# Putting off three quarters of the first-level picks, and putting the low weight part on the one-hots with ScalarE

## The chip, the core and the metric

The kernel runs on one core of one Trainium2 chip. The metric is the device time of one execution in microseconds. Three executions of the kernel before gave 1546.49 (median), 1546.44 and 1548.01 us.

## The reference, cut to what matters

One encoder layer over 512 tokens of width 1024: attention (two kinds), a LayerNorm, and a retrieval feed-forward (PEER) beside a gated embedding, then a second LayerNorm. The change is in the feed-forward:

```python
q = (xb @ w_q).reshape(PEER_CHUNK, PEER_HEADS, PEER_KEY_DIM)
s1 = jnp.einsum('thd,kd->thk', q[..., :half], sub_keys[0])
s2 = jnp.einsum('thd,kd->thk', q[..., half:], sub_keys[1])
v1, i1 = lax.top_k(s1, PEER_TOPK)
v2, i2 = lax.top_k(s2, PEER_TOPK)
cand = (v1[..., :, None] + v2[..., None, :]).reshape(PEER_CHUNK, PEER_HEADS, PEER_TOPK * PEER_TOPK)
cv, ci = lax.top_k(cand, PEER_TOPK)
...
g = jax.nn.softmax(cv.astype(jnp.float32), axis=-1).reshape(PEER_CHUNK, -1).astype(xb.dtype)
u = u_table[idx]
hpre = jnp.einsum('td,ted->te', xb, u)
act = g * jax.nn.gelu(hpre, approximate=False)
return jnp.einsum('te,ted->td', act, v_table[idx])
```

There are 8 heads, 128 sub-keys on each of two sides, 16 picks for each head, and 16384 experts; so every token has 128 experts with a weight each.

## The kernel before, in words

The 512 tokens are four chunks of 128: chunk 0, chunk 1 (`NGC`), chunks 2 and 3. Chunk 0 gathers its experts' rows by indirect DMA (GpSimd issues them). Chunks 1 to 3 become a dense matrix of weights (token by expert), which is multiplied with all of the value table; the activations of chunks 2 and 3 come from dense "lead" products with the u table (`lead_block`, L1156), those of chunk 1 from gathered rows (`own_rows`).

The stages around the change, in order:

- **Query stage.** For each of 16 groups g (a head and a side), TensorE projects all tokens (L113 to L115) and scores them against the 128 sub-keys (`sub_scores`, L849). ScalarE copies the scores of the four chunks out in one instruction (L858), and VectorE picks the 16 best for each chunk at once (`top16`, L831: five instructions, called a pick below; 64 picks in all).
- **Lead stage.** TensorE works through a fixed list, `gate_and_leads`: 100 lead blocks of 8 matmuls and, among the first, 16 gate steps of 12. VectorE, meanwhile: `route(1)` (second-level picks and the indices), `route(2)`, `build_g(2)`, `route(3)`, `build_g(3)`, `route(0)`, `build_g(1)`. The 128 gathered rows of chunk 1 (`own_rows`, L1071: one instruction each on 128x1024, the gather five buffers ahead, L1069) are strewn between the steps from `route(2)` on, and 26 rows of chunk 0 (`beside`) among and after `build_g(1)`.
- **build_g** turns a chunk's picks into dense weights. Three transposes (L993) on TensorE bring indices and weights into place, and VectorE copies them out (L997). Then there are 16 steps of 8 tokens. VectorE makes the one-hots of both indices (L1041) and multiplies one of them by the weight's upper and lower 16-bit part (L1052, two instructions); TensorE multiplies the pairs (L1016), ScalarE copies the sums out (L1028, two instructions). Every fourth step ScalarE issues a write of 2 MB to DRAM (L1033): 12 writes over the three builds.
- **Value stage.** 128 blocks, each read, cut in two parts and multiplied with the weights (L1389), beside the other gathers of chunk 0.

All five engines follow an order that is fixed while the program is recorded. The vector steps `yield` an amount of us; `run` gives that amount times `PACE` (1.1) of lead work to TensorE (`run_pe`) and times `OWN` of gathered rows to VectorE. So the amounts decide which lead matmuls stand ahead of which transposes in TensorE's list, and the gate's lower parts (`g_lo`, L1185) stand in VectorE's list where the lead work called for them. The one-hot tiles (`oh_i`, `oh_j`) have two buffers.

Of the kernel before, what the change touches and what calls it, by code (L numbers as in the profile page):

```python
# [9 lines left out]
F32 = mybir.dt.float32  # L10
F32R = mybir.dt.float32r
I32 = mybir.dt.int32
F16 = mybir.dt.float16
U32 = mybir.dt.uint32
AF = mybir.ActivationFunctionType
OP = mybir.AluOpType
# [17 lines left out]
GT = 32  # L34
GB = 8
LEAD = 100
SPILL = 88
KEPT = 8
FIRST = 8
PACE = 1.1  # L40
AHEAD = 14.0
LAG = 6.0
BESIDE = 26
PRE = BESIDE
OWN = 1.2
OWN_G = 0.7
OWN_G_LATE = 4.0
SEAM = 7.0
# [3 lines left out]
OT = 8  # L52
G_UP = 32768.0
# [18 lines left out]
def tile_encoder_layer(ctx: ExitStack, tc: tile.TileContext, A: dict, out: bass.AP):  # L72
    nc = tc.nc
# [18 lines left out]
    def r32(ap):  # L92
        return ap.bitcast(F32)
# [748 lines left out]
    gb = rw.tile([128, D], F32, name="gb")  # L842
    for k in range(8):
        nc.gpsimd.tensor_tensor(whole[:, k, :], r32(hTh[:, k, ts]), r32(hTl[:, k, ts]), op=OP.add)
    pQ = ExitStack()
    rq = pQ.enter_context(tc.tile_pool(name="rq", bufs=1, reuse_waits="tile"))
    skT = rq.tile([128, 2, 128], F32, name="skT")
    nc.sync.dma_start(skT, A["skT"])
    def sub_scores(g, ps):  # L849

        qT = rq.tile([128, 512], F32, name="q_t", bufs=2)
        nc.scalar.copy(qT, ps)
        pt = ps_tile("tr")
        for c in range(4):
            nc.tensor.matmul(pt[:, c * 128:(c + 1) * 128], qT[:, c * 128:(c + 1) * 128], skT[:, g % 2, :],
                             start=True, stop=True)
        s = rq.tile([128, 4, 128], F32, name="sc", bufs=3)
        nc.scalar.copy(s, pt.rearrange("p (c k) -> p c k", c=4))  # L858
        for c in range(4):
            tmp = rq.tile([128, 128], F32, name="tk_t", bufs=2)  # L860
            top16(v_all[:, c, g // 2, g % 2], i_all[:, c, g // 2, g % 2], s[:, c, :], tmp)

    first = []
    for g in range(16):
# [20 lines left out]
        sub_scores(g, ps)  # L885
    pQ.close()

    pb = ExitStack()
    bt = pb.enter_context(tc.tile_pool(name="bt", bufs=2, side="right", reuse_waits="tile"))
    bs = [pb.enter_context(tc.tile_pool(name=f"bs{x}", bufs=1, side="right", reuse_waits="tile")) for x in range(2)]  # L890
    rg = pR.enter_context(tc.tile_pool(name="rg", bufs=1, reuse_waits="tile"))

    def route(c, res):
# [93 lines left out]
    def build_g(c, e1, e2, gw):  # L987
# [9 lines left out]
        nc.vector.tensor_copy(eT.rearrange("p q s t -> p s q t"),  # L997
                              ps[:, 0:256].rearrange("p (s q t) -> p s q t", s=2, t=OT))
        yield 0.4
        wT = bt.tile([128, 2, 128], F16, name="wT")  # L1000
        nc.scalar.mul(wT[:, 0], ps[:, 256:384], G_UP)
        nc.vector.scalar_tensor_tensor(wT[:, 1], ps[:, 256:384], G_UP, wT[:, 0], op0=OP.mult, op1=OP.subtract)
        yield 0.3
        wide = [128, OT // 2, 128, 2]

        def in_pairs(x):
            return x.rearrange("p (a b) -> p a b", b=2).unsqueeze(2)
# [29 lines left out]
        for q in range(128 // OT):  # L1037
            t0 = OT * q

            om = bt.tile([128, 2, OT // 2, 128, 2], F16, name="oh_i")  # L1040
            nc.vector.tensor_tensor(om.rearrange("p s a j b -> p (s a) j b"),  # L1041
                                    iota2.unsqueeze(1).to_broadcast([128, OT, 128, 2]),
                                    in_pairs(eT[:, q].rearrange("p s t -> p (s t)")).to_broadcast([128, OT, 128, 2]),
                                    op=OP.is_equal)
            if ahead:
                sums = products(*ahead)
                due -= 1.3
            yield 1.2

            ow = bt.tile([128, 2, OT // 2, 128, 2], F16, name="oh_j")  # L1050
            for x in range(2):
                nc.vector.tensor_tensor(ow[:, x], om[:, 1], in_pairs(wT[:, x, t0:t0 + OT]).to_broadcast(wide),  # L1052
                                        op=OP.mult)
                if not x:
                    yield 0.65
            if ahead:
                leave(ahead[0], sums)
            ahead = (q, om, ow)
            yield 0.65
        sums = products(*ahead)  # L1060
# [216 lines left out]
    with tc.manual_schedule(engines={nc.vector.engine, nc.scalar.engine, nc.tensor.engine, nc.sync.engine,  # L1277
                                     nc.gpsimd.engine}):
        for _ in range(RAWS):
            load_u()  # L1280
        held = []
        run(route(NGC, held))
        own = own_rows(*held)
        run_pe(next(own))
        own_due = -OWN_LATE
        for c in range(NGC + 1, 4):
            res = []
            run(route(c, res), OWN)
            if c > NGC + 1:
                run_pe(WAIT)  # L1290
            run(build_g(c, *res), OWN)
        lead0 = route(0, [])
        for _ in range(14):
            run([next(lead0)], OWN)
        own_due = 1e9
        run([0.0], 1.0)
        for _ in own:
            pass
        own = None
        run_pe(LAG)  # L1300

        first_g = pX.tile([128, NTG, GB, GT], F32, name="gt1")
        nc.sync.dma_start(first_g[:, 128 // GT:].rearrange("p g i t -> p g (i t)"),
                          g_dram[128 // GT:, :, SPILL * GT:(SPILL + GB) * GT].rearrange("g p x -> p g x"))
        build = build_g(NGC, *held)
        next(build)
        run(lead0)
        own = beside()
        own_due = -OWN_G_LATE
        run(build, OWN_G)  # L1310
        for x in own:
            run_pe(x)
        pb.close()
# [247 lines left out]
```

## Time and profile before

| | |
|---|---|
| median of the runs | 1546.49 us |
| profiled execution, its time | 1548.03 us |
| profiled execution, its span | 1545.9 us |
| mean granted TensorE clock | 0.98 of full speed |
| TensorE busy | 1472.0 us (95%) |
| VectorE busy | 1291.7 us (84%) |
| ScalarE busy | 551.0 us (36%) |
| GpSimd busy | 581.2 us (38%) |
| moved by DMA | 459.34 MB |

Busy shares are means over stages with different limits; the stage that the change touches runs from about 412 us (the first lead matmul) to about 913 us. What is 2 us longer than the span is the start and the end around it. DMA "share" is the mean busy share of 16 DMA engines.

### The profile page before, as it was taken

The numbers are of one execution on the slowest core, as the hardware profiler recorded it, in microseconds if no ns is written. First come the engines' busy times: TensorE is split into PE (matmuls) and PEld (weight loads), VectorE is DVE, ScalarE is ACT, GpSimd is POOL, SyncE is SP. The second block draws the span as 40 slices with busy tenths as digits, with TensorE's granted clock in tenths as the row PEclk, the third lists the DMA queues.
The fourth block names the chain that finished last, engine by engine and source line by source line (L and its number), as shares of the span: only waits on it lengthen the run. The fifth ranks groups of instructions, "written<-read, shape, count | busy, mean of one in ns | idle before, by whom it ended". The sixth has DMA issues, their size and how long they took to land.

```text
span 1545.9 us, 22318 instructions
## 1 busy us (share of the span) xinstructions
PE 1472.0 (95%) x7747; PEld 1219.7 (79%) x7747; DVE 1291.7 (84%) x2737; ACT 551.0 (36%) x938; POOL 581.2 (38%) x520
## 2 busy tenths in 40 slices
PE   9999899999999998998799969999999999999997
PEld 5788777788888887887688747888887888887785
DVE  7376685679889987888688978999998999989996
ACT  3355685333222222212222223434433333333332
POOL 1013110010015434354422454556555666665620
PEclk9999999999999999999999979999999999999999
DMA  6343240143379999999998999999999999999982
GB/s 228 99 113 96 79 123 28 48 139 91 106 240 344 344 394 392 403 412 398 405 357 309 411 379 369 405 403 395 406 400 394 396 395 395 396 395 397 392 329 82
DMA packets 194213, 459.34 MB, mean 297 GB/s; under 512 B 18226, under 2 KB 97970, under 8 KB 192564
## 3 DMA queue, kind: packets, MB, share of 16 engines
q1 hardware_dynamic: 121712, 214.08, 38.5%
q0 software_dynamic: 57984, 207.12, 34.9%
q10 hardware_dynamic: 14404, 36.71, 6.0%
q8 instruction: 61, 1.00, 0.3%
q14 instruction: 52, 0.43, 0.1%
HBM read 414.07 MB, written 40.89 MB: 294 GB/s over the span
## 4 chain that ended last, share of the span: by engine, by line
PE 37%; DMA 25%; DVE 13%; issue 13%; POOL 8%; ACT 2%; SPq 1%; POOLq 0%; DVEq 0%; ACTq 0%
PE acc L1389 10%; DMA v_raw<-in_v_rows_dram 8%; DMA gt<-g_dram 5%; DMA raw<-in_v_rows_dram 4%; PE pj L113 3%; POOL whi L1069 3%; PE pj L114 3%; PE pj L115 3%; PE mm L113 3%; POOL wlo L1069 3%; DMA whi<-in_u_rows_dram,s_ix 3%; PE mm L115 3%; PE mm L114 3%; DMA ge<-ge_dram 2%; PE hp L1156 2%
## 5 line engine op out<-in xcount | busy, mean ns | idle before, releaser
L1372 POOL DMA_INDIRECT gat<-in_v_rows_dram,i_sel x128 | 212.7, 1661 | 135.3 <-DVE base L1374 114.3
L1156 PE MATMUL mm<-whole,raw 128*128 128x256 f32 x880 | 206.5, 390 | 1.3 <-DMA raw<-in_uT_dram 1.3
L1156 PEld LDWEIGHTS mm<-whole,raw 128*128 128x128 f32 x880 | 169.3, 196 | 24.4 <-ACT ge L1138 1.6
L98 ACT CAST whi<-raw 128x1024 fp32r<-128x1024 f32 (+4 forms) x117 | 117.3, 1003 | 163.3 <-DMA raw<-in_v_rows_dram 54.8
L1357 POOL DMA_INDIRECT gat<-in_u_rows_dram,i_sel x102 | 134.1, 1314 | 108.1 <-DVE hdot L1363 85.8
L1374 DVE SCALAR_TENSOR_TENSOR base<-gat,hdot,base 128x1024 f32<-128x1024 f32 x128 | 163.8, 1280 | 1.6
L99 DVE TENSOR_TENSOR wlo<-raw,whi 128x1024 fp32r<-128x1024 f32 (+4 forms) x117 | 135.4, 1158 | 32.9 <-ACT whi L98 32.6
L1389 PE MATMUL acc<-v_hi,a_hi 128*128 128x512 f32 x480 | 150.1, 393 | 6.4 <-ACT a_hi L98 6.4
L1389 PE MATMUL acc<-v_lo,a_hi 128*128 128x512 f32 x480 | 149.2, 391 | 0.2
L1389 PE MATMUL acc<-v_hi,a_lo 128*128 128x512 f32 x480 | 148.5, 390 | 0.0
L1069 POOL DMA_INDIRECT whi<-in_u_rows_dram,s_ix x51 | 62.5, 1225 | 195.3 <-DVE cand L910 131.9
L98 ACT CAST v_hi<-v_raw 128x1024 fp32r<-128x1024 f32 x80 | 84.0, 1051 | 137.3 <-DMA v_raw<-in_v_rows_dram 51.9
L1363 DVE CUSTOM_DVE_ANT_0 scr<-gat,h 128x1024 f32<-128x1024 f32 x102 | 124.6, 1222 | 2.2
L98 ACT CAST a_hi<-gt 128x384 fp32r<-128x384 f32 x126 | 64.5, 512 | 160.4 <-DVE gt L1438 102.5
L1389 PEld LDWEIGHTS acc<-v_hi,a_hi 128*128 128x128 f32 x480 | 87.5, 188 | 26.4 <-ACT a_hi L98 9.4
L1389 PEld LDWEIGHTS acc<-v_lo,a_hi 128*128 128x128 f32 x480 | 89.7, 188 | 21.0 <-DVE v_lo L99 2.0
L1389 PEld LDWEIGHTS acc<-v_hi,a_lo 128*128 128x128 f32 x480 | 89.6, 188 | 19.7 <-DVE a_lo L99 0.9
L1389 PE MATMUL acc<-whi,a_hi 128*128 128x512 f32 x276 | 90.0, 408 | 15.2 <-ACT a_hi L98 15.2
L99 DVE TENSOR_TENSOR a_lo<-gt,a_hi 128x384 fp32r<-128x384 f32 x126 | 69.5, 552 | 41.7 <-ACT a_hi L98 41.7
L99 DVE TENSOR_TENSOR v_lo<-v_raw,v_hi 128x1024 fp32r<-128x1024 f32 x80 | 97.4, 1217 | 7.9 <-ACT v_hi L98 7.9
L1069 POOL DMA_INDIRECT wlo<-in_u_rows_dram,s_ix x51 | 63.1, 1237 | 85.2 <-DVE s_dot L1071 73.8
L1389 PE MATMUL acc<-whi,a_lo 128*128 128x512 f32 x276 | 88.5, 401 | 0.0
(393 smaller groups left out, 3359.9 us busy)
## 6 DMA issues: line engine op xcount, KB each, us to landing
raw<-in_uT_dram SPq DMA_DIRECT2D x104, 512.0 KB, 7.5
v_raw<-in_v_rows_dram SPq DMA_DIRECT2D x82, 512.0 KB, 10.0
g_dram<-g_st ACTq DMA_DIRECT2D x12, 2048.0 KB, 11.7
gt<-g_dram SPq DMA_DIRECT2D x60, 384.0 KB, 14.3
raw<-in_v_rows_dram SPq DMA_DIRECT2D x44, 512.0 KB, 12.5
raw_u<-in_uT_dram SPq DMA_DIRECT2D x24, 512.0 KB, 7.4
ge_dram<-ge ACTq DMA_DIRECT2D x88, 128.0 KB, 7.2
ge<-ge_dram SPq DMA_DIRECT2D x88, 128.0 KB, 12.7
```

The lines of the kernel that those rows point to most:

```text
L98: nc.scalar.copy(hi, src)
L99: nc.vector.tensor_tensor(lo, src, r32(hi), op=OP.subtract)
L113: nc.tensor.matmul(ps, a[0], b[0], start=start, stop=False)
L114: nc.tensor.matmul(ps, a[0], b[1], start=False, stop=False)
L115: nc.tensor.matmul(ps, a[1], b[0], start=False, stop=stop)
L1069: nc.gpsimd.indirect_dma_start(out=u[:], out_offset=None, in_=u_rows, in_offset=bass.IndirectOffsetOnAxis(ap=ix[:, k:k + 1], axis=0))
L1156: nc.tensor.matmul(ps[:, :N_U], raw[:, k], whole[:, k, :], start=(k == 0), stop=(k == 7))
L1357: nc.gpsimd.indirect_dma_start(out=u[:], out_offset=None, in_=u_rows, in_offset=bass.IndirectOffsetOnAxis(ap=i_sel[:, c, k:k + 1], axis=0))
L1363: nc.vector.tensor_tensor_reduce(scr, u, h[c], op0=OP.mult, op1=OP.add, accum_out=hdot[:, c, k:k + 1], scale=1.0, scalar=0.0)
L1372: nc.gpsimd.indirect_dma_start(out=u[:], out_offset=None, in_=v_rows, in_offset=bass.IndirectOffsetOnAxis(ap=i_sel[:, c, k:k + 1], axis=0))
L1374: nc.vector.scalar_tensor_tensor(base[c], u, hdot[:, c, k:k + 1], base[c], op0=OP.mult, op1=OP.add)
L1389: nc.tensor.matmul(acc[c][hf], a[:, cs], b[:, hf * 512:(hf + 1) * 512], start=(n == 0 and i == 0), stop=(n == 127 and i == 2))
```

## The change

Four things are changed. (1) In the query stage the scores are copied out in two instructions: those of chunk 0 into a long-lived buffer (`later`, which is a staging tile of the builds), those of chunks 1 to 3 together; the last four groups of these go into the same buffer. VectorE picks chunk 1 at once, and chunks 2 and 3 of the first 12 groups one group later. The 16 picks of chunk 0 and the last four of chunks 2 and 3 (24 of 64) are put off. (2) These are made in the lead stage: four ahead of `route(2)`, twenty (16 of chunk 0, four of chunk 3) ahead of `build_g(2)`, each with an amount of 1.7. (3) In a build step VectorE multiplies by the upper part alone; ScalarE multiplies the same one-hot by the lower part, token by token, 8 instructions of 128x128 with a scale for each partition. (4) `OWN` goes from 1.2 to 1.0. Two pools are opened earlier.

```diff
-OWN = 1.2
+OWN = 1.0
+LATE_G = 12
...
-        s = rq.tile([128, 4, 128], F32, name="sc", bufs=3)
-        nc.scalar.copy(s, pt.rearrange("p (c k) -> p c k", c=4))
-        for c in range(4):
-            tmp = rq.tile([128, 128], F32, name="tk_t", bufs=2)
-            top16(v_all[:, c, g // 2, g % 2], i_all[:, c, g // 2, g % 2], s[:, c, :], tmp)
+        pt = pt.rearrange("p (c k) -> p c k", c=4)
+        nc.scalar.copy(later[:, g], pt[:, 0])
+        if g < LATE_G:
+            s = rq.tile([128, 3, 128], F32, name="sc", bufs=3)
+        else:
+            s = later[:, 16 + 3 * (g - LATE_G):19 + 3 * (g - LATE_G)]
+        nc.scalar.copy(s, pt[:, 1:4])
+        pick(NGC, g, s[:, NGC - 1])
+        for c in range(NGC + 1, 4):
+            if g < LATE_G:
+                others.append((c, g, s[:, c - 1]))
+            else:
+                left[c].append((c, g, s[:, c - 1]))
+        left[0].append((0, g, later[:, g]))
+        while others and (others[0][1] < g or g == 15):
+            pick(*others.pop(0))
+
+    def picks(c):
+        for x in left[c]:
+            pick(*x)
+            yield 1.7
...
-        wT = bt.tile([128, 2, 128], F16, name="wT")
-        nc.scalar.mul(wT[:, 0], ps[:, 256:384], G_UP)
-        nc.vector.scalar_tensor_tensor(wT[:, 1], ps[:, 256:384], G_UP, wT[:, 0], op0=OP.mult, op1=OP.subtract)
+        wT = bt.tile([128, 128], F16, name="wT")
+        nc.scalar.mul(wT, ps[:, 256:384], G_UP)
+        wl = bt.tile([128, 128], F32, name="wl")
+        nc.vector.scalar_tensor_tensor(wl, ps[:, 256:384], G_UP, wT, op0=OP.mult, op1=OP.subtract)
...
-            for x in range(2):
-                nc.vector.tensor_tensor(ow[:, x], om[:, 1], in_pairs(wT[:, x, t0:t0 + OT]).to_broadcast(wide),
-                                        op=OP.mult)
-                if not x:
-                    yield 0.65
+            nc.vector.tensor_tensor(ow[:, 0], om[:, 1], in_pairs(wT[:, t0:t0 + OT]).to_broadcast(wide), op=OP.mult)
             if ahead:
                 leave(ahead[0], sums)
+            for t in range(OT):
+                nc.scalar.mul(ow[:, 1, t // 2, :, t % 2], om[:, 1, t // 2, :, t % 2], wl[:, t0 + t:t0 + t + 1])
...
             res = []
+            run(picks(c), OWN)
             run(route(c, res), OWN)
             if c > NGC + 1:
                 run_pe(WAIT)
+            else:
+                run(picks(0), OWN)
+                run(picks(c + 1), OWN)
+                left[c + 1] = []
             run(build_g(c, *res), OWN)
```

Three places of the order are shown. First TensorE's list at the transposes of `build_g(2)` (L993, in the changed file L1018), before:

```order
L1156 MATMUL hp<-whole,raw_u 128x256 x8
L1156 MATMUL hp<-whole,raw 128x256 x5
L993 MATMUL tr<-ident,e_4870 128x128
L993 MATMUL tr<-ident,e_5009 128x128
L993 MATMUL tr<-ident,gw 128x128
L1156 MATMUL hp<-whole,raw 128x256 x11
L113 MATMUL mm<-g_hi,hTh 128x512
L114 MATMUL mm<-g_lo,hTh 128x512
```

and in the changed kernel:

```order
L1180 MATMUL hp<-whole,raw 128x256 x16
L1180 MATMUL hp<-whole,raw_u 128x256 x8
L1180 MATMUL mm<-whole,raw 128x256 x24
L1180 MATMUL mm<-whole,raw_u 128x256 x8
L1180 MATMUL mm<-whole,raw 128x256
L1018 MATMUL tr<-ident,e_4845 128x128
L1018 MATMUL tr<-ident,e_5034 128x128
L1018 MATMUL tr<-ident,gw 128x128
L1180 MATMUL mm<-whole,raw 128x256 x20
L1042 LDWEIGHTS oh_j
L1042 MATMUL tr<-oh_i,oh_j 128x128
```

Before, 133 lead matmuls and 96 gate matmuls stand ahead of these transposes; now 321 and all 192. Ahead of the transposes of `build_g(3)` it was 435 lead matmuls and is 547, ahead of those of `build_g(1)` 707 and 758 of the 800.

Second VectorE's list in `build_g(3)` (s_dot marks a gathered row), before:

```order
L997 CAST eT<-tr 128x2x16x8
L1002 SCALAR_TENSOR_TENSOR wT<-tr,wT 128x128
L1071 ISA whi,s_dot<-whi,h_s 128x1024
L1071 ISA s_dot 128x1
L1041 TENSOR_TENSOR oh_i<-iota_3277,eT 128x2048
L1071 ISA wlo,s_dot<-wlo,h_s 128x1024
L1071 ISA s_dot 128x1
L1052 TENSOR_TENSOR oh_j<-oh_i,wT 128x1024 x2
```

and now:

```order
L1022 CAST eT<-tr 128x2x16x8
L1028 SCALAR_TENSOR_TENSOR wl<-tr,wT 128x128
L1095 ISA whi,s_dot<-whi,h_s 128x1024
L1095 ISA s_dot 128x1
L1067 TENSOR_TENSOR oh_i<-iota_3277,eT 128x2048
L1095 ISA wlo,s_dot<-wlo,h_s 128x1024
L1095 ISA s_dot 128x1
L1077 TENSOR_TENSOR oh_j<-oh_i,wT 128x1024
L1067 TENSOR_TENSOR oh_i<-iota_3277,eT 128x2048
```

The second multiplication is gone. Over the whole list 45 rows of chunk 1 now stand ahead of the first build (14 before), 25 and 24 in the first two builds (39 each before), and behind the last multiplication of `build_g(1)` stand 11 rows of chunk 0 (5 before).

Third ScalarE's list at the start of `build_g(2)`, before:

```order
L1001 ACTIVATE wT<-tr 128x128
L1184 CAST g_hi<-g_raw 128x512
L1138 ACTIVATE ge<-hp 128x256
L1140 DMA ge_dram<-ge 128x256
L1184 CAST g_hi<-g_raw 128x512
L1028 ACTIVATE g_st<-tr 128x128x4 x2
L1138 ACTIVATE ge<-hp 128x256
```

and now:

```order
L1026 ACTIVATE wT<-tr 128x128
L1162 ACTIVATE ge<-mm 128x256
L1164 DMA ge_dram<-ge 128x256
L1081 ACTIVATE oh_j<-oh_i,wl 128x128 x8
L1162 ACTIVATE ge<-mm 128x256
L1164 DMA ge_dram<-ge 128x256
L1054 ACTIVATE g_st<-tr 128x128x4 x2
L1081 ACTIVATE oh_j<-oh_i,wl 128x128 x8
```

Each step's eight multiplications stand behind the copies of the step before it.

## Rows read from the trace of the kernel before

**Rows 1.** The page's first line.
```profile
span 1545.9 us, 22318 instructions
```

**Rows 2.** Windows: busy us and instructions by engine, TensorE clock, DMA share, GB/s.
```profile
412.00:598.00 186.00, 183.78 (x987) 157.05 (x986) 166.28 (x416) 48.87 (x95) 68.25 (x54) 1.00 0.90 329
598.00:828.00 230.00, 209.94 (x1150) 182.56 (x1150) 182.38 (x411) 47.49 (x99) 95.21 (x78) 0.96 0.98 380
828.00:913.00 85.00, 66.55 (x465) 56.51 (x464) 72.21 (x108) 28.21 (x55) 35.83 (x30) 0.89 0.99 389
925.00:1500.00 575.00, 564.24 (x2764) 470.76 (x2763) 532.89 (x699) 212.71 (x292) 329.19 (x217) 1.00 1.03 395
```

**Rows 3.** Windows of 10 us, the same columns.
```profile
590.00:600.00 10.00, 9.13 (x55) 7.77 (x53) 6.63 (x12) 2.23 (x5) 4.94 (x4) 1.00 1.02 425
810.00:820.00 10.00, 10.00 (x48) 8.81 (x47) 9.55 (x18) 4.08 (x7) 0.00 (x0) 1.00 0.67 200
820.00:830.00 10.00, 10.00 (x50) 8.79 (x49) 4.12 (x10) 1.30 (x4) 4.71 (x5) 1.00 0.77 250
```

**Rows 4.** The query stage: a window, and VectorE's timeline at one pick.
```profile
330.00:410.00 80.00, 80.00 (x400) 66.10 (x400) 76.67 (x425) 25.07 (x36) 0.00 (x0) 1.00 0.27 80
...
330.76 0.29 DVE L832 MAX8 v_all<-sc 128x8 f32<-128x128 f32 x1
331.93 1.23 DVE L99 TENSOR_TENSOR wlo<-raw,whi 128x1024 fp32r<-128x1024 f32 x1
```

**Rows 5.** VectorE's timeline in `route(1)`: a wait.
```profile
444.46 0.69 DVE L1185 TENSOR_TENSOR g_lo<-g_raw,g_hi 128x512 fp32r<-128x512 f32 x1 [3.09 <-ACT g_hi L1184]
```

**Rows 6.** TensorE: timeline (each lead matmul is two records), and the builds' transposes.
```profile
412.15 1.02 PE L1156 MATMUL hp<-whole,raw 128*128 128x256 f32 x4
...
570.56 4.10 PE L1156 MATMUL mm<-whole,raw 128*128 128x256 f32 x18
574.50 1.08 PE L1016 MATMUL tr<-oh_i,oh_j 128*128 128x128 f16 x16
...
L993 PEld LDWEIGHTS tr<-ident,e x4: 139/142/143, 492.9 to 673.5; 128*128 128x128 f32 x4
```

**Rows 7.** VectorE's waits for gathered rows, 420 to 913 us: total, times, longest.
```profile
DVE wlo L1071 <- DMA wlo<-in_u_rows_dram,s_ix: 20.6, 12, 5.2
DVE whi L1071 <- DMA whi<-in_u_rows_dram,s_ix: 16.5, 12, 3.7
DVE row L1071 <- DMA row<-in_u_rows_dram,s_ix: 9.8, 10, 3.0
```

**Rows 8.** VectorE's timeline in `build_g(2)`, and where the value stage begins.
```profile
539.70 0.68 DVE L1052 TENSOR_TENSOR oh_j<-oh_i,wT 128x1024 f16<-128x1024 f16 x1
540.30 1.22 DVE L1071 CUSTOM_DVE_ANT_0 wlo<-wlo,h_s 128x1024 f32<-128x1024 f32 x1
...
541.44 1.22 DVE L1041 TENSOR_TENSOR oh_i<-iota,eT 128x2048 f16<-128x2048 f16 x1
542.58 1.22 DVE L1071 CUSTOM_DVE_ANT_0 whi<-whi,h_s 128x1024 f32<-128x1024 f32 x1
...
912.55 0.56 DVE L99 TENSOR_TENSOR a_lo<-gt,a_hi 128x384 fp32r<-128x384 f32 x1 [9.66 <-ACT a_hi L98]
```

**Rows 9.** ScalarE's groups by shape: busy us, mean ns, idle before.
```profile
L468 ACT ACTIVATE p_t<-pj,gk 128x512 f32<-128x512 f32 x2 | 1.4, 685 | 0.0
L470 ACT ACTIVATE p_exp<-pj 128x512 f32<-128x512 f32 x2 | 1.2, 590 | 0.0
L1001 ACT ACTIVATE wT<-tr 128x128 f16<-128x128 f32 x3 | 0.8, 277 | 5.1 <-DVE eT L997 4.7 <-ACT ge L1138 0.4
L1028 ACT ACTIVATE g_st<-tr 128x512 f32<-128x512 f32 x96 | 52.5, 595 | 56.1 <-PE tr L1016 51.2 <-ACT ge L1138 4.8
```

**Rows 10.** The builds' writes: all 12 (first and last start), and the third.
```profile
L1033 ACTq DMA_DIRECT2D g_dram<-g_st x12: 326/326/327, 532.7 to 895.9; - x12
...
589.68 0.33 ACTq L1033 DMA_DIRECT2D g_dram<-g_st  x1
```

More of the change, by code (lines that the diff above doesn't have):

```diff
@@ L844, in tile_encoder_layer @@
         nc.gpsimd.tensor_tensor(whole[:, k, :], r32(hTh[:, k, ts]), r32(hTl[:, k, ts]), op=OP.add)
+    pb = ExitStack()
+    bt = pb.enter_context(tc.tile_pool(name="bt", bufs=2, side="right", reuse_waits="tile"))
+    bs = [pb.enter_context(tc.tile_pool(name=f"bs{x}", bufs=1, side="right", reuse_waits="tile")) for x in range(2)]
     pQ = ExitStack()
@@ L856, in sub_scores, with pick @@
                              start=True, stop=True)
-        s = rq.tile([128, 4, 128], F32, name="sc", bufs=3)
-        nc.scalar.copy(s, pt.rearrange("p (c k) -> p c k", c=4))
-        for c in range(4):
-            tmp = rq.tile([128, 128], F32, name="tk_t", bufs=2)
-            top16(v_all[:, c, g // 2, g % 2], i_all[:, c, g // 2, g % 2], s[:, c, :], tmp)
+        pt = pt.rearrange("p (c k) -> p c k", c=4)
[14 more added lines that the diff above has]
+            pick(*others.pop(0))
+    def pick(c, g, src):
+        tmp = rt.tile([128, 128], F32, name="tk_t", bufs=2)
+        top16(v_all[:, c, g // 2, g % 2], i_all[:, c, g // 2, g % 2], src, tmp)
+    def picks(c):
+        for x in left[c]:
+            pick(*x)
+            yield 1.7
+    later = bs[1].tile([128, 128, GT], F32, name="g_st").rearrange("p i t -> p (i t)").rearrange(
+        "p (n k) -> p n k", k=128)
+    others, left = [], [[], [], [], []]
     first = []
@@ L886, in tile_encoder_layer @@
     pQ.close()
-    pb = ExitStack()
-    bt = pb.enter_context(tc.tile_pool(name="bt", bufs=2, side="right", reuse_waits="tile"))
-    bs = [pb.enter_context(tc.tile_pool(name=f"bs{x}", bufs=1, side="right", reuse_waits="tile")) for x in range(2)]
     rg = pR.enter_context(tc.tile_pool(name="rg", bufs=1, reuse_waits="tile"))
```

## The prediction

> **What bounds the kernel now.** I read the windows first, then VectorE's waits, then the timelines at the places that the change touches. The sum is made against the profiled execution, 1548.0 us (span 1545.9 [rows 1]); the median of the runs, 1546.5, is 1.5 us lower, and the last step carries the difference over to it. A measurement of this kernel can tell about 0.2%, 3.1 us, from no change.
>
> The query stage is TensorE's: busy 80.00 of 80 us, VectorE 76.67 beside it [rows 4]. The lead stage falls in two. From 412 to 598 us TensorE is busy 183.8 of 186 us and its list sets the pace. From 598 to 913 it is busy 276.5 of 315, VectorE 254.6 and ScalarE 75.7, while the DMA engines have a share of 0.98 to 0.99 [rows 2]; at best they moved 425 GB/s, the mean is 380 to 389 [rows 2, 3]. VectorE's waits say the same: 46.9 us for gathered rows of chunk 1 [rows 7], and 9.7 us before it goes on at 912.5 [rows 8]. So behind 598 us it is the transfers that are late. The value stage has all of TensorE, VectorE and DMA nearly full (564 and 533 of 575 us, share 1.03 [rows 2]); its lists are unchanged, and I leave its length alone, so the question is when it begins: before, with that resumption at 912.5 us.
>
> **The start.** Behind the last scores VectorE had four picks, now one before `route(1)`: three times 1.17 us (from one pick's start to the end of its five instructions [rows 4]), 3.5 us sooner. That is lost at once: `route(1)` waits at 444.46 for ScalarE's upper part of a gate weight [rows 5], which needs the first gate matmuls done, and TensorE's list is the same up to there. The wait of 3.1 becomes 6.6. The query stage gets no shorter, since TensorE bounds it; the second score copy lies in ScalarE's idle time (25 of 80 busy [rows 4]). Term: 0, at most 3.5 us gained.
>
> **VectorE's own sum is nearly nothing.** Put off: 24 picks of 1.17 = 28.1 us, moved from a stage where TensorE covers them into the lead stage. Taken away: 48 multiplications of 0.60 us (start to start [rows 8]) = 28.8 us.
>
> **What is moved on TensorE counts.** A lead matmul costs 3.94 us / 9 = 0.438 us [rows 6]. The first transposes came at 492.9, behind 133 lead matmuls and 96 gate matmuls that began at 412.15 [rows 6]: (80.75 - 133 x 0.438) / 96 = 0.234 us for a gate matmul. Now 321 and 192 stand ahead: 140.6 + 44.9 = 185.5, so the transposes of `build_g(2)` come at about **597.7 us**, and no engine can bring them sooner. VectorE's list up to there is 45 rows of 1.14 us [rows 8] and 24 picks, 79.4 us, where before it did in the same time 49 rows (54 gathers [rows 2], five ahead) and 12 build steps (the third write is issued at 589.7 [rows 10]) of 1.14 + 2 x 0.60 us: 84.0 us. It was busy 166 of 186 us; so it now idles some 20 + 4.6 = 24 us before the transposes.
>
> Behind 598 the engines have about what they had. TensorE: 479 lead matmuls and 48 steps of at most 1.08 us [rows 6], 262 us, as before but for 12 steps. VectorE: 109 rows and 48 steps of 1.74 us against 105 rows and 36 steps of 2.34, 207.8 against 203.9, the rest equal: 254.6 + 4 = 259 us. Neither fills 315.
>
> **The transfers are what is late.** A gather is 128 x 1024 x 4 bytes = 0.524 MB, a build's write 2.097 MB. By 598 the kernel before had issued 54 gathers and 3 writes, the changed one 50 and none; the lead blocks are equal. 4 x 0.524 + 3 x 2.097 = 8.4 MB, and as the end of the third write was still under way, I take **8 MB** more left. From 598 to 912.5 the kernel before moved 230 x 0.380 + 84.5 x 0.389 = 120.3 MB; now 128.3. Bounds: always at 425 GB/s takes 301.9 us, plus the hole at 810 to 830 (225 GB/s instead of 425, 9.4 us [rows 3]), which stays, since `route(0)` must end before chunk 0's gathers can begin: 909.3, or 3 us sooner than 912.5. At the old mean rate, 382.5, it takes 335.4 us: 933.4, 21 us later. The old stretch had 314.5 - 283.1 = 31.4 us of slack against 425 GB/s, 9.4 of it that hole, 22 elsewhere. Of the 22 I keep 9, two fifths: two routes lie behind 598 as before, and in the builds rows and writes ask for more than 425 GB/s in either kernel (25 rows, 14 lead blocks of 0.655 MB with their result and 8.4 MB of writes for 56 us of VectorE's list). So 909.3 + 9 = 918: **6 us late**.
>
> **ScalarE** gets 384 small multiplications, 8 in a step. No row has 128x128 with a scale for each partition. The nearest is 0.277 us with a constant scale; 128x512 takes 0.685 with a scale for each partition and 0.590 without, 0.095 more; and two copies of 0.595 lie in 52.5 / 48 = 1.09 us, an overlap of 0.10 [rows 9]. Upper end 0.277 + 0.095 = 0.37, lower end 0.277 - 0.10 = 0.18; I take 0.27, between them and next to 0.277. A step is then 8 x 0.27 + 1.09 = 3.25 us, a build 52, and with ScalarE's other work (48.9 us of 186 [rows 2], less the copies of 12 steps, 13: 0.19 us for each us) 64 us. The transfers of a build (13.1 + 9.2 + 8.4 = 30.7 MB) need 72 us at 425 GB/s. So ScalarE is hidden under them, by 8 us; at 0.37 it needs 80 and is not. Term: 0, at most 8 us for each of the first two builds and 10 for the last.
>
> **Sum:** 1548.0 + 6 = 1554.0 for the profiled execution, **1552.5 us** as a median. Start, pools and the later place of chunk 1's reload on SyncE's queue: 0, all under the transfers.
>
> **The rivals.** *The last build gives back more than the delay* (faster). VectorE's 16 steps there are 9.6 us shorter, and behind the last multiplication stand 11 rows instead of 5, 6.8 us more work while the last write (issued at 895.9 [rows 10]) lands: the wait of 9.7 shrinks to about 3. Together 16.5 us; begun 6 to 7 us late, the value stage starts 10 us early: 1536.5. For it: VectorE is 72 of 85 us busy there [rows 2]. Against it: the 33 MB of those 84.5 us would have to pass in 68, 485 GB/s. It decides if the eight gathers issued ahead for the value stage (4.2 MB) and some value rows fall behind the start, when 400 GB/s are enough; and if ScalarE ends the build in under 60 us.
>
> *The DMA engines fill up* (no change): of the 22 us of slack a fifth or less is left, and it ends within 3 us of 912.5: 1546.5. For it: 425 GB/s were reached in the midst of a build [rows 3].
>
> *ScalarE binds* (slower still): 0.37 us for each small multiplication makes the builds 80 us, and the one-hots' two buffers hold VectorE to that: 2 x 8 + 10 = 26 us on top, 1578. It decides from 0.32 us on, where a build reaches 72 us. Against it: small instructions overlapped in rows 9. The Trainium skill's page "ScalarE: Activation LUTs" (section "Rules for kernel authors") gives plain multiplications to VectorE rather than ScalarE, as up to about three times faster in bf16. By this rule the edit is wrong wherever ScalarE is the later engine; the rows agree on the ratio (0.60 us against 8 x 0.27 = 2.2 us), and if three times held here exactly, 1.8 us a step, ScalarE would stay hidden.
>
> That the early start does nothing is part of my forecast; if it does work, its 3.5 us don't pass the transposes at 597.7, since TensorE's list holds these.
>
> **How the numbers follow.** My forecast (transfers late, 6 us) 0.40; the last build gives back more 0.32; no change 0.20; ScalarE binds 0.08. Faster by over 0.2% is 0.32, within 0.2% 0.20, slower 0.48. My own case alone runs from 1549 to 1567 (the old mean rate). The range over all cases: down to 1535, 1.5 us under the first rival, up to 1570, which leaves out most of the last; 1535 to 1570. Most of the chance lies close to no change, on both sides.
>
> **What the profile after would show.** The first transposes (L1018) at 595 to 601 us, with VectorE idle over 15 us before them for TensorE (or, before that, for the gate's upper parts): if they come by 585, the list is not what holds them. The first build write about 17 us later. From 598 on DMA at 395 GB/s or more and each of the first two builds 68 to 80 us long. The small multiplications start 0.25 to 0.30 us apart; over 0.32 speaks for ScalarE. The last transposes near 838 us, and VectorE's resumption near 918; if the last stretch takes under 75 us between the two, the first rival has it. What would make the forecast wrong most simply is that the waits for gathered rows fall to under 30 us without a change in GB/s: then bytes were never the limit, but how soon the gathers were asked for.

## The result, and the profile after

The changed kernel takes 1563.81 us (median of four runs, 1561.91 to 1565.67) against 1546.72 us for the kernel before in the same comparison: a ratio of 1.0109, 95% interval 1.0091 to 1.0126, so 17 us slower. The forecast was 1552.5 us, range 1535 to 1570: right in direction, 11 us short in size. Ratios and intervals, here and below, leave out one slow execution of e8 (2091.93 us at a granted clock of 0.654), and they are not quotients of the medians. The profiled execution has a span of 1561.7 us, 15.8 more than before [rows 1].

The windows that answer to [rows 2] (busy us and instructions of TensorE, its weight loads, VectorE, ScalarE and GpSimd, then TensorE's granted clock, DMA share, GB/s):

```profile
412.00:598.00 186.00, 185.27 (x844) 158.61 (x843) 159.77 (x525) 36.31 (x73) 57.73 (x50) 1.00 0.86 306
598.00:828.00 230.00, 215.98 (x1338) 183.09 (x1337) 190.98 (x410) 133.16 (x379) 101.03 (x78) 1.00 1.01 404
828.00:913.00 85.00, 66.20 (x402) 43.63 (x400) 64.76 (x98) 58.95 (x176) 33.16 (x27) 0.77 0.84 308
925.00:1500.00 575.00, 562.19 (x2746) 469.17 (x2745) 529.06 (x701) 209.05 (x287) 342.96 (x226) 0.99 1.03 394
```

Between 598 and 828 TensorE and the DMA engines both do more than before. Between 828 and 913 TensorE is busy as long as before, at a lower clock, and the DMA engines do less. Over both together, before and after, the rate is much the same:

```profile
598.00:913.00 315.00, 276.50 (x1612) 239.06 (x1612) 254.58 (x519) 75.69 (x154) 131.04 (x108) 0.94 0.98 382
598.00:913.00 315.00, 282.18 (x1738) 226.71 (x1736) 255.74 (x507) 192.11 (x555) 134.19 (x105) 0.94 0.96 378
```

The line numbers of the changed kernel are other ones: transposes L1018, small multiplications L1081, evictions L1054, writes L1059, gathered rows L1095. TensorE's and ScalarE's rows by line (duration min/median/max in ns, first and last start), for [rows 6, 10]:

```profile
L1018 PE MATMUL tr<-ident,e x4: 272/272/273, 598.3 to 723.1; 128*128 128x128 f32 x4
L1018 PE MATMUL tr<-ident,e1s x1: 273/273/273, 840.4 to 840.4; 128*128 128x128 f32 x1
...
L1059 ACTq DMA_DIRECT2D g_dram<-g_st x12: 326/326/327, 620.6 to 903.3; - x12
...
L1081 ACT ACTIVATE oh_j<-oh_i,wl x384: 417/428/453, 602.6 to 901.8; 128x128 f16<-128x128 f16 x192
```

The transposes of the first build stand at 598.3 us, those of the last at 840.4 (827.9 before). VectorE's waits from 420 to 913 us, for [rows 5, 7]:

```profile
DVE whi L1095 <- DMA whi<-in_u_rows_dram,s_ix: 12.0, 10, 2.3
DVE g_lo L1209 <- ACT g_hi L1208: 11.8, 7, 3.3
DVE row L1095 <- DMA row<-in_u_rows_dram,s_ix: 9.5, 6, 3.2
DVE wlo L1095 <- DMA wlo<-in_u_rows_dram,s_ix: 9.2, 11, 2.6
```

The waits for chunk 1's rows fell from 46.9 to 30.7 us. And VectorE's timeline where the value stage begins, for [rows 8]:

```profile
906.88 1.29 DVE L1095 CUSTOM_DVE_ANT_0 whi<-whi,h 128x1024 f32<-128x1024 f32 x1 [1.08 <-DMA whi<-in_u_rows_dram,i_sel]
...
915.66 1.23 DVE L1095 CUSTOM_DVE_ANT_0 wlo<-wlo,h 128x1024 f32<-128x1024 f32 x1 [7.48 <-DMA wlo<-in_u_rows_dram,i_sel]
...
921.13 1.23 DVE L1095 CUSTOM_DVE_ANT_0 whi<-whi,h 128x1024 f32<-128x1024 f32 x1 [0.41 <-DMA whi<-in_u_rows_dram,i_sel]
...
926.03 0.56 DVE L100 TENSOR_TENSOR a_lo<-gt,a_hi 128x384 fp32r<-128x384 f32 x1 [0.58 <-ACT a_hi L99]
```

It resumes at 926.03 instead of 912.55. So of the 15.8 us of span, 12.5 were lost up to the last transposes, 1.0 between these and the resumption (85.6 us against 84.6), and 2.3 in the value stage (635.7 against 633.4).

### The profile page after: what moved, and what is told of

Its sections match the earlier page's. It is cut to its first block, busy times and chain, and to the rows that moved or that the text cites. A ratio compares the mean times of both kernels' runs of the same rounds, so it can differ in the third digit from the quotient of the medians.

```text
span 1561.7 us, 22711 instructions
## 1 busy us (share of the span) xinstructions
PE 1484.6 (95%) x7747; PEld 1212.8 (78%) x7747; DVE 1273.6 (82%) x2689; ACT 660.9 (42%) x1338; POOL 584.8 (37%) x520
## 4 chain that ended last, share of the span: by engine, by line
PE 53%; DMA 17%; DVE 12%; issue 9%; ACT 4%; POOL 4%; SPq 0%; POOLq 0%; DVEq 0%; ACTq 0%
PE acc L1418 16%; PE mm L1180 6%; PE hp L1180 4%; DMA raw<-in_v_rows_dram 4%; DMA ge<-ge_dram 4%; PE mm L114 3%; PE mm L116 3%; PE mm L115 3%; PE pj L114 3%; PE pj L115 3%; PE pj L116 3%; DMA v_raw<-in_v_rows_dram 2%; DMA gt<-g_dram 2%; DMA whi<-in_u_rows_dram,s_ix 2%; POOL whi L1093 2%
## 5 line engine op out<-in xcount | busy, mean ns | idle before, releaser
L1180 PE MATMUL mm<-whole,raw 128*128 128x256 f32 x880 | 201.4, 381 | 2.5 <-DMA raw<-in_uT_dram 2.2
L1180 PEld LDWEIGHTS mm<-whole,raw 128*128 128x128 f32 x880 | 164.6, 191 | 24.4 <-issue 3.2
L1081 ACT ACTIVATE oh_j<-oh_i,wl 128x128 f16<-128x128 f16 x384 | 119.0, 429 | 6.9 <-DVE oh_i L1067 3.4
L1418 PEld LDWEIGHTS acc<-v_hi,a_hi 128*128 128x128 f32 x480 | 88.0, 189 | 29.9 <-ACT a_hi L99 11.8
L1418 PEld LDWEIGHTS acc<-v_lo,a_hi 128*128 128x128 f32 x480 | 90.0, 188 | 20.8 <-DVE v_lo L100 1.1
L1042 PE MATMUL tr<-oh_i,oh_j 128*128 128x128 f16 x768 | 74.0, 232 | 20.0 <-DVE oh_j L1077 12.4
```

What stands on the lines that cost most here:

```text
L1081: nc.scalar.mul(ow[:, 1, t // 2, :, t % 2], om[:, 1, t // 2, :, t % 2], wl[:, t0 + t:t0 + t + 1])
L1180: nc.tensor.matmul(ps[:, :N_U], raw[:, k], whole[:, k, :], start=(k == 0), stop=(k == 7))
L1418: nc.tensor.matmul(acc[c][hf], a[:, cs], b[:, hf * 512:(hf + 1) * 512], start=(n == 0 and i == 0), stop=(n == 127 and i == 2))
```

## The experiments

The kernel before took 1545.9 to 1549.2 us (medians) beside these runs. In each experiment, "last transposes" means the first of them.

**Which part costs.** First each part was undone, which also changes the amounts that set the order. e1 is the kernel before with this:

```diff
-OWN = 1.2
+OWN = 1.0
...
-        wT = bt.tile([128, 2, 128], F16, name="wT")
-        nc.scalar.mul(wT[:, 0], ps[:, 256:384], G_UP)
-        nc.vector.scalar_tensor_tensor(wT[:, 1], ps[:, 256:384], G_UP, wT[:, 0], op0=OP.mult, op1=OP.subtract)
+        wT = bt.tile([128, 128], F16, name="wT")
+        nc.scalar.mul(wT, ps[:, 256:384], G_UP)
+        wl = bt.tile([128, 128], F32, name="wl")
+        nc.vector.scalar_tensor_tensor(wl, ps[:, 256:384], G_UP, wT, op0=OP.mult, op1=OP.subtract)
...
-            for x in range(2):
-                nc.vector.tensor_tensor(ow[:, x], om[:, 1], in_pairs(wT[:, x, t0:t0 + OT]).to_broadcast(wide),
-                                        op=OP.mult)
-                if not x:
-                    yield 0.65
+            nc.vector.tensor_tensor(ow[:, 0], om[:, 1], in_pairs(wT[:, t0:t0 + OT]).to_broadcast(wide), op=OP.mult)
...
+            for t in range(OT):
+                nc.scalar.mul(ow[:, 1, t // 2, :, t % 2], om[:, 1, t // 2, :, t % 2], wl[:, t0 + t:t0 + t + 1])
```

> Parts 1 and 2 undone: every pick stands in the query stage as before, and only the low part of the weights is ScalarE's. Theory A (the put-off picks move the builds back on TensorE's list, and with them gathers and writes): 120 lead and 96 gate matmuls stand ahead of the first transposes again, so these come at 485 to 495 us, the last ones at 815 to 828, and the time is 1538 to 1548 us. Theory B (ScalarE's 8 small multiplications a step pace the builds, wherever these stand): first transposes as early, but the last ones still at 835 or later and the time 1556 to 1564 us.

Measured: 1560.08 us, ratio 1.009 (1.0062 to 1.0118), as theory B had the time. But the last transposes started at 790.1, sooner than either theory had it, and the third of them, which needs the weighted rows, at 809.9; TensorE had waited 19.4 us for these. And 74 lead matmuls stood behind the last product and ran until 922.7 us, and the value stage waited for them. Without the second multiplication's amount the list calls for too few leads. The list can err the other way too, and this run doesn't tell what ScalarE costs.

e2 is the changed kernel with the part on `wT` and `ow` of that diff turned back.

> Part 3 undone: the low part is VectorE's again (two multiplications a step), the picks stay put off. Theory A: first transposes at about 598 us as in the changed kernel; VectorE now has 28.8 us more behind them, so the last ones come at 840 to 860 and the time is 1564 to 1580 us. Theory B: a build step falls from 3.35 us to about 2.5, the last stretch (last transposes to VectorE's resumption) gets 8 us or more shorter and the time is under 1556 us.

Measured: 1577.91 us, 1.0197 (1.0169 to 1.0225); transposes at 599.2 and 859.6. As theory A had it in numbers, but the reason may lie in the list again: with the 0.65 back, 800 lead matmuls (all) stand ahead of the last transposes instead of 758. 42 x 0.438 [rows 6] = 18.4 us, and 859.6 - 840.4 = 19.2.

So the parts were then tried with the order held fixed. e5, ScalarE's part alone in the old order, is e1 with two lines more:

```diff
-OWN = 1.0
+OWN = 1.2
...
             nc.vector.tensor_tensor(ow[:, 0], om[:, 1], in_pairs(wT[:, t0:t0 + OT]).to_broadcast(wide), op=OP.mult)
+            yield 0.65
```

> The kernel before with nothing but the low part of the weights on ScalarE; every amount that sets the order is kept, so that 133, 435 and 707 lead matmuls stand ahead of the three builds' transposes as before. Theory D (what made the changed kernel late is the order that the changed amounts give: transposes behind more lead matmuls, and too few of these left for the last build): the last transposes at 815 to 828 us, the time 1538 to 1549 us. Theory B (ScalarE at 3.35 us a step, against 2.34 us of VectorE's list, is late in every build): rows, transposes and end all come later, 1553 us or more.

Measured: 1550.62 us, 1.0017 (0.9999 to 1.0035): no difference that can be told. The rows of this run (transposes and writes by line, VectorE's timeline at the resumption):

```profile
L993 PE MATMUL tr<-ident,e1s x1: 272/272/272, 819.9 to 819.9; 128*128 128x128 f32 x1
...
L1034 ACTq DMA_DIRECT2D g_dram<-g_st x12: 326/326/327, 532.1 to 897.0; - x12
...
913.45 0.56 DVE L99 TENSOR_TENSOR a_lo<-gt,a_hi 128x384 fp32r<-128x384 f32 x1 [11.80 <-ACT a_hi L98]
```

VectorE's saving brings the last transposes 8 us forward; the last build, 77 us from there to its last write instead of 68, gives them back. In the old order ScalarE's part has no gain or price that can be told. (The same work in e1's order: 1560.08 us, 1.009.) The other way round, picks put off, the low part on VectorE, and the new order kept: e10 is e2 without an amount for the second multiplication.

```diff
             for x in range(2):
                 nc.vector.tensor_tensor(ow[:, x], om[:, 1], in_pairs(wT[:, x, t0:t0 + OT]).to_broadcast(wide),
                                         op=OP.mult)
-                if not x:
-                    yield 0.65
```

> The changed kernel with the low part back on VectorE and every amount of the list as changed, so that the same 321, 547 and 758 lead matmuls stand ahead of the three transposes. Theory A (the list and the transfers hold, whoever multiplies): last transposes at 838 to 845 us, the time 1560 to 1568. Theory B (ScalarE is what made the changed kernel slower): the time under 1555 us. If VectorE's 28.8 us are wanted after all in this order, last transposes at 850 or later and over 1572 us.

Measured: 1566.79 us, 1.0125 (1.0104 to 1.0145); last transposes at 845.8. Theory A, 0.8 us late at the transposes. Giving ScalarE's work back to VectorE doesn't help: the loss is with the picks, or with the new order. (A price of ScalarE's could hide here behind VectorE's 28.8 us; e4 below takes half of ScalarE's work away without giving it to VectorE.) And e10 and e2 do the same work and differ in that one amount: with 42 more lead matmuls ahead of the last transposes these came 13.8 us later, and the time was 11 us longer (1.0197 against 1.0125).

**The picks' work, or their place in the list.** e11: all picks back in the query stage, their steps in the list left empty.

```diff
-            if g < LATE_G:
-                others.append((c, g, s[:, c - 1]))
-            else:
+            others.append((c, g, s[:, c - 1]))
+            if g >= LATE_G:
                 left[c].append((c, g, s[:, c - 1]))
+        others.append((0, g, later[:, g]))
...
         for x in left[c]:
-            pick(*x)
             yield 1.7
```

> The changed kernel with all picks back in the query stage (those of chunk 0 too), while the put-off ones keep their places and amounts in the list as empty steps: TensorE's list is that of the changed kernel, 321, 547 and 758 lead matmuls ahead of the three transposes, and VectorE has 28 us less to do in the lead stage. Theory L (the list holds: TensorE reaches the transposes late because so many lead matmuls stand ahead, whatever VectorE does): first transposes at 596 to 600, last ones at 832 to 841 us, the time 1555 to 1563 us. Theory V (the 28 us on VectorE are what costs): gathers and rows are asked sooner, the last transposes come by 828 and the time is 1545 to 1551 us.

Measured: 1566.0 us, 1.0123 (1.0086 to 1.016). With 28 us less for VectorE to do in the lead stage, the kernel is as slow as the changed one. The rows (a window, then transposes):

```profile
412.00:598.00 186.00, 185.28 (x847) 158.86 (x846) 131.90 (x377) 36.27 (x74) 58.13 (x50) 1.00 0.87 313
...
L1017 PE MATMUL tr<-ident,e x4: 272/272/273, 597.1 to 725.1; 128*128 128x128 f32 x4
...
L1017 PE MATMUL tr<-ident,e1s x1: 273/273/273, 844.6 to 844.6; 128*128 128x128 f32 x1
```

VectorE is busy 131.9 us instead of 159.8 and idles for the rest; TensorE, as full as ever, reaches the transposes at the same place. Theory L, at the slow end or beyond: 844.6 was outside its 832 to 841, and the time 3 us above its 1555 to 1563. With e10 and e2 it puts the loss down to the order. The new order with both moves of work undone at once wasn't run.

e12, the same picks once more:

```diff
             pick(*x)
+            pick(*x)
             yield 1.7
```

> The changed kernel with every put-off pick done twice over (the same numbers again), with no more amount in the list: VectorE has 28 us more in the lead stage, TensorE's list is the same. Theory V: VectorE reaches the first transposes 20 to 28 us later, at 615 to 626, and the time is 1578 to 1592 us. Theory L (VectorE's waits of 23 us ahead of 598 take up most of the 28): first transposes by 606 and the time 1562 to 1570 us.

Measured: 1590.74 us, 1.0268 (1.023 to 1.0306); transposes at 610.3 and 865.7. Between the two at the first transposes, and theory V in the time. In the changed kernel VectorE and TensorE come to the first transposes together (VectorE waits 2.8 us there), so more work on VectorE does cost, though less doesn't gain.

e6, the opposite: the picks put off, but the list as it was before.

```diff
-OWN = 1.0
+OWN = 1.2
...
-            yield 1.7
+            yield 0.0
...
             nc.vector.tensor_tensor(ow[:, 0], om[:, 1], in_pairs(wT[:, t0:t0 + OT]).to_broadcast(wide), op=OP.mult)
+            yield 0.65
```

> The changed kernel with the order of the kernel before: the put-off picks count nothing in the list (0 instead of 1.7 each), the place of the removed multiplication still counts 0.65, OWN is 1.2. All three parts of the change work, and TensorE's list is that of the kernel before. Theory D: the first transposes wait for VectorE, which has 24 picks (28 us) more ahead of them, and come at 510 to 525 us, the last ones at 815 to 828, the time is 1536 to 1549 us. Theory B: 1553 us or more. If the picks themselves cost (VectorE's sum), this one is 5 us or more above the run with ScalarE's part alone.

Measured: 1587.21 us, 1.0251 (1.0213 to 1.0289); transposes at 497.1, sooner than theory D's 510, and 854.9, later than its 828. Theory D falls, and theory B has the time for a reason that it doesn't name; the third sentence holds, the picks themselves cost, 37 us above e5. They stand in VectorE's list ahead of gate work that TensorE's list soon needs (TensorE's waits from 412 to 960 us):

```profile
PE mm L114 <- DVE base L1228: 30.0, 1, 30.0
```

e7 has `yield 0.4` there, OWN at 1.0 and the same `yield 0.65`.

> The changed kernel with an order in between: a put-off pick counts 0.4 instead of 1.7, the place of the removed multiplication still counts 0.65, OWN stays 1.0; 168, 441 and 732 lead matmuls stand ahead of the three transposes, and 20 rows instead of 14 before the last build's end. Theory D: between the other two orders, first transposes at 520 to 535 us, 1542 to 1553 us. Theory B: 1553 us or more.

Measured: 1569.49 us, 1.0162 (1.0125 to 1.0199); transposes at 539.6 and 845.0. Not between the kernels before and after, as theory D said (theory B has the time), but between the old list with the late picks and the changed kernel. Of the three amounts tried for a late pick (0, 0.4 and 1.7, the first two with the 0.65), the change's own 1.7 costs least.

**Are the transfers late?** e9: the 8.4 MB of the first build's writes taken out of the time behind 598 us.

```diff
-                nc.scalar.dma_start(g_dram[g], stage.rearrange("p i t -> p (i t)"))
+                if c != NGC + 1:
+                    nc.scalar.dma_start(g_dram[g], stage.rearrange("p i t -> p (i t)"))
...
+        for g in range(128 // GT, 256 // GT):
+            for k in range(2):
+                nc.scalar.dma_start(g_dram[g][:, k * 2048:(k + 1) * 2048], whole.rearrange("p k t -> p (k t)"))
```

> Left out: the write of the first build's four blocks; in their place 8.4 MB of other numbers are written to the same place before the lead stage, where the DMA engines are little used, so that only when the bytes pass is changed (the output is off by the first build's share). Theory A as predicted (from 598 us on the transfers are what is late): the last transposes come 10 to 16 us sooner than in the changed kernel, at 824 to 830, which is where TensorE's own list ends up; the time is 1548 to 1556 us. Rival (TensorE's list or ScalarE sets the pace from 598 to 840): last transposes within 3 us of 840, the time 1559 to 1565.

Measured: 1562.44 us, 1.0085 (1.0056 to 1.0114). A window and the last transposes:

```profile
598.00:828.00 230.00, 221.41 (x1354) 188.09 (x1353) 196.56 (x424) 133.36 (x381) 100.70 (x79) 0.99 0.98 371
...
L1018 PE MATMUL tr<-ident,e1s x1: 273/273/273, 837.9 to 837.9; 128*128 128x128 f32 x1
```

The rate falls from 404 to 371 GB/s, and the last transposes come 2.5 us sooner, where the bytes at 404 GB/s are worth 20.8. The rival: TensorE is now busy 221 of 230 us. From 598 to 841 VectorE's waits for gathered rows fell from 27.5 to 15.5 us, and even that brought no more. Up to the last transposes the transfers weren't what was late.

**ScalarE's price, and the last build.** e4, beside the products left out:

```diff
-            for t in range(OT):
+            for t in range(OT // 2):
                 nc.scalar.mul(ow[:, 1, t // 2, :, t % 2], om[:, 1, t // 2, :, t % 2], wl[:, t0 + t:t0 + t + 1])
```

> Left out: the low part of tokens 4 to 7 of each step, that is 4 of ScalarE's 8 small multiplications and the products that read them; the output differs by these terms. Theory B (ScalarE paces): a step falls from 3.35 to about 2.2 us; all three builds get shorter, the time is 1545 to 1553 us. Theory A with C: the first two builds hang on transfers and rows, not on ScalarE, so the last transposes stay within 4 us of 840; only the last stretch gains, at most 5 us: 1557 to 1563 us.

Measured: 1559.17 us, 1.008 (1.0051 to 1.0108). Theory A with C in the first two builds: last transposes at 837.6, 242 us behind the first as in the changed kernel, though TensorE had 8.6 us less to do as well; the last build took 52 us to its last write (889.6) instead of 63, yet VectorE resumed only 24 us behind that write. The stretch from last transposes to resumption was 76 us, 9 shorter and not 5 at most.

e3, in the changed kernel:

```diff
-OWN_G = 0.7
+OWN_G = 1.0
```

> One number: in the last build the rows of chunk 0 come 1.0 us per us of the build's list instead of 0.7, so that 3 or 4 of them are left behind it instead of 11. Theory C (in the last stretch the gathers are asked too late, since the rows follow the list's amounts while the build runs at ScalarE's pace): the stretch falls from 86 us to 76 to 80 and the time to 1554 to 1558 us. Rival (the stretch is set by the transfers' bytes or by ScalarE's own work): it stays 84 to 87 us and the time at 1561 to 1566.

Measured: 1562.37 us, 1.0079 (1.0053 to 1.0105). Its writes and resumption:

```profile
L1059 ACTq DMA_DIRECT2D g_dram<-g_st x12: 326/326/330, 621.1 to 906.7; - x12
...
923.36 0.56 DVE L100 TENSOR_TENSOR a_lo<-gt,a_hi 128x384 fp32r<-128x384 f32 x1 [10.44 <-ACT a_hi L99]
```

The stretch from the last transposes (840.6) is 82.8 us, 2.8 shorter: between theory C and the rival, and the rival has the time. The rows put into the build made it 3.2 us longer; from its last write it is then 16.7 us to the resumption, as before (895.9 to 912.55 [rows 8, 10]), instead of 22.7.

e8 is e5 with VectorE doing the low part where `c == NGC`, the last build; `wT` has two parts there.

```diff
+                part = wT[:, x] if c == NGC else wT
+                if not x or c == NGC:
+                    nc.vector.tensor_tensor(ow[:, x], om[:, 1], in_pairs(part[:, t0:t0 + OT]).to_broadcast(wide),
+                                            op=OP.mult)
...
+            for t in range(OT if c != NGC else 0):
                 nc.scalar.mul(ow[:, 1, t // 2, :, t % 2], om[:, 1, t // 2, :, t % 2], wl[:, t0 + t:t0 + t + 1])
```

> The order of the kernel before, the low part on ScalarE in the first two builds only; in the last one VectorE does it as before. Theory E (value rows resume about 16.5 us behind the last write of the builds, and from the last transposes to that write it is 68 us with VectorE's low part but 77 with ScalarE's): last transposes at 817 to 824 us, last write at 885 to 892, VectorE's resumption at 901 to 908, the time 1537 to 1543 us. Rival (transfers fix the last write, whoever multiplies): last write at 894 to 898 as in the kernel before, 1545 to 1551 us.

Measured: 1549.15 us, 1.001 (0.9996 to 1.0024). Last transposes at 823.0, then:

```profile
L1039 ACTq DMA_DIRECT2D g_dram<-g_st x12: 326/326/327, 532.1 to 892.2; - x12
...
906.48 0.56 DVE L99 TENSOR_TENSOR a_lo<-gt,a_hi 128x384 fp32r<-128x384 f32 x1 [7.77 <-ACT a_hi L98]
```

Theory E held as far as the start of the value stage, 6 us sooner than before, but the kernel ended no sooner: its value stage took 641.8 us against 633.4. Half of those 8 us went at once: by 945 us e8 was only 1.8 us ahead, as VectorE had waited 6.06 us for ScalarE and ScalarE 8.11 us for a row still in transfer. The rest went bit by bit up to the end; why wasn't tried. No version here beats the kernel before.

## Why the prediction was right, and where it was wrong

**The start** (term 0). Held, by a slightly different way: VectorE did come to `route(1)` sooner, by 2.7 us, and lost it at an earlier gate weight, at 432.49 (a wait of 2.71 us); the wait at 444 stayed at 3.3 instead of growing to 6.6. **VectorE's sum is nearly nothing** held as arithmetic and misled as a measure: taking 28.8 us away was worth nothing (e5), adding 28.1 costs 37 us in one order (e6 against e5), and in the changed order taking them away again gains nothing (e11). What an engine's time is worth depends on who waits at that place.

**The first transposes at 597.7 us** held within 1 us (598.3). VectorE was to idle some 24 us before them, and did idle 26 (186 - 159.8), but strewn ahead of them, 11.8 for the gate's upper parts, with only 2.8 at the transposes themselves: total idle time is not slack at the place that counts, as e12 shows. The first write came 22.3 us behind them (17 forecast), the first two builds took 77 and 74 us to their last write (68 to 80 forecast), and the last transposes, "near 838", held within 3. But all that was forecast from 598 on rests on a step that failed: **"The transfers are what is late"**, with "Behind 598 the engines have about what they had ... Neither fills 315" ahead of it. I took 598 to 913 us as one stretch, and TensorE's 276 busy us of 315 looked like room. That the kernel came out slower, and the last transposes so near 838, was luck as far as the mechanism goes: the 6 us were for bytes that, as e9 shows for the stretch up to there, nobody was late for. The stretch falls in two at the last transposes. 707 lead matmuls stood ahead of these before, 758 in the changed kernel. The table works out the time from the first lead matmul on with the forecast's own prices (0.438 us for a lead matmul, 0.234 for each of 192 gate matmuls, 1.08 for each of the 32 steps of the first two builds); the last column is what is left of the measured time:

| kernel | leads ahead | worked out | measured to the last transposes | left |
|---|---|---|---|---|
| before | 707 | 389.2 | 415.7 | 26.5 |
| after | 758 | 411.5 | 428.0 | 16.5 |
| e5, low part alone | 707 | 389.2 | 408.3 | 19.1 |
| e10, new list, low part on VectorE | 758 | 411.5 | 433.5 | 22.0 |
| e11, new list, picks early | 758 | 411.5 | 433.2 | 21.7 |
| e9, 8.4 MB less | 758 | 411.5 | 424.6 | 13.1 |
| e2, e10 with the 0.65 back | 800 | 429.9 | 446.3 | 16.4 |

Most of what is left are TensorE's waits for VectorE's one-hots, here before (493 to 828 us) and after (598 to 841 us); the rest is other waits and a lower clock:

```profile
PE tr L1016 <- DVE oh_j L1052: 18.8, 8, 4.2
PE tr L1042 <- DVE oh_j L1077: 10.8, 8, 2.8
```

51 more matmuls are 22.3 us; what is left became 10.0 shorter; 12.3 us remain, and 12.5 were measured. Where VectorE is short of time more is left (36 in e7, 43 in e12, 56 in e6). In the new list either move of work could be undone without a gain (e10, e11), and the 8.4 MB taken away gave 2.5 us of the 20.8 (e9). That it is the matmuls ahead, and not the places of the rows in VectorE's list, which the amounts move too, rests on this sum; no run moved the matmuls alone. My test "if the waits for gathered rows fall to under 30 us without a change in GB/s" was all but met: 30.7 us, and from 598 to 913 us 378 GB/s against 382. The 404 GB/s up to 828 hide that: a high rate showed that transfers were under way, not that anyone was late for them. The second rival (the DMA engines fill up, no change) had the rate right up to 828 only (308 GB/s behind it), and fell for the same reason.

**Behind the last transposes** only 42 lead matmuls are left instead of 93, 22 us of TensorE's work less beside a build that doesn't need TensorE so much. There they cost nothing that shows (84.6 us with them, 85.6 without); ahead of the transposes they do. TensorE waits more and more, and four windows of 10 us of the changed kernel show it:

```profile
880.00:890.00 10.00, 7.46 (x46) 2.94 (x46) 7.57 (x12) 9.97 (x30) 3.02 (x3) 0.54 0.69 254
890.00:900.00 10.00, 7.80 (x48) 3.24 (x48) 8.72 (x13) 10.00 (x31) 4.31 (x4) 0.50 0.99 368
900.00:910.00 10.00, 2.33 (x15) 1.02 (x15) 6.12 (x12) 3.65 (x11) 8.06 (x6) 0.50 0.98 329
910.00:920.00 10.00, 0.00 (x0) 0.00 (x0) 4.21 (x7) 0.53 (x1) 2.87 (x3) 0.50 1.00 412
```

ScalarE is full until 900. The forecast had 80 us from there to the resumption (838 to 918) and it took 85.6: the term that was mis-sized second. The build itself was shorter, 62.9 us to its last write instead of 68.0, in good part for its rows were left behind it (3.2 us by e3); with them it took 22.7 us from that write to the resumption instead of 16.7.

**The first rival** (the last build gives back more) had the rows behind the build filling a wait of VectorE's. They did, but they came late (7.48 us for one at 915.66), probably since their gathers are asked only five ahead, and e3 shows that putting them into the build makes that stretch 2.8 us shorter, not 16. **ScalarE binds**: in the last build a step took 3.3 us, or 3.6 with a lead block's copy (`ge`) in it, where I had 3.25. Eight small multiplications start 0.29 us apart (0.27 forecast):

```profile
865.61 1.06 ACT L1054 ACTIVATE g_st<-tr 128x512 f32<-128x512 f32 x2
866.56 2.48 ACT L1081 ACTIVATE oh_j<-oh_i,wl 128x128 f16<-128x128 f16 x8
868.90 0.37 ACT L1162 ACTIVATE ge<-mm 128x256 f32<-128x256 f32 x1
869.16 1.07 ACT L1054 ACTIVATE g_st<-tr 128x512 f32<-128x512 f32 x2
```

That is 2.34 us for what VectorE does in 0.60 [rows 8]; in e5 it lengthens the last build alone. The Trainium skill's page "ScalarE: Activation LUTs" (section "Rules for kernel authors") gives multiplications to VectorE as up to about three times faster for each element, in bf16 and with one source. Measured, in fp16 and with two sources on VectorE, it is 3.9 times, but that is eight instructions against one; and e5 shows that in the old order it decides nothing by itself.

**The value stage**, which I left alone, took 2.3 us more. That is less than it differs between the experiments (633 to 646 us in their profiled executions, and 658 in e1, where leads ran into it).

## What to carry to other kernels

Where an order is laid down by amounts, a step's amount is part of its price: the changed amounts put 188 more lead matmuls ahead of the first transposes and 51 ahead of the last, and in that list the kernel stayed 1.2% slower with the moved picks taken out again; 42 matmuls more, with the same work for every engine, cost another 11 us (e2 against e10). Cut a stretch at every point that others wait for before saying that an engine has room in it, and ask what stands ahead of that point, not what the engine is busy with on the whole. And test a limit by taking its load away: a full queue is no proof that it is the one awaited.

## What the runs showed of the hardware

A 128x128 multiplication with a scale for each partition takes 428 ns on ScalarE by its own record, but eight in a row start 293 ns apart: the durations alone would have made a step 1.1 us too long. The Trainium skill's page "ScalarE: Activation LUTs" (section "What ACT_TABLE_LOAD costs") states about 280 ns and 0.833 ns for each element with one operand for each partition, and an overlap of about 93 ns; the estimate from it, 294 ns from start to start, agrees with the 293, while its 387 ns for one by itself is less than the 428 recorded here.

Gaps of TensorE cost twice: in the run with doubled picks it waited 9.45 us, the granted clock fell (windows, columns as above), and the first 16 small matmuls behind the wait took 1.89 us, against 1.08 for the same 16 some 5 us later (timeline):

```profile
620.00:630.00 10.00, 1.08 (x11) 1.08 (x12) 9.93 (x21) 3.27 (x11) 5.90 (x5) 0.64 0.72 254
630.00:640.00 10.00, 10.00 (x69) 8.77 (x68) 10.00 (x16) 8.37 (x24) 6.22 (x5) 0.85 0.94 333
...
628.92 1.89 PE L1043 MATMUL tr<-oh_i,oh_j 128*128 128x128 f16 x16 [9.45 <-DVE oh_j L1078]
...
634.01 1.08 PE L1043 MATMUL tr<-oh_i,oh_j 128*128 128x128 f16 x16
```

The changed kernel had no such dip there (1.00 in the first block of rows above); the half-low run, e4, had one (0.96 from 598 to 841), which may be why its 8.6 us fewer matmuls brought the transposes no closer together. That was not tried by itself. In the last build of the changed kernel the clock stood at 0.50, the lower level of 1.2 GHz, from 890 to 920 us: at first with TensorE busy 7.80 of 10 us in bursts of small matmuls, then with nothing to do. It was back at 1.00 from 930.
